# Feed-forward block of an encoder layer: TensorE's and SyncE's orders fixed in the second product, last sends behind its first loads, the block's pool split in three

## The chip, the cores and the metric

The kernel runs on one core of a Trainium2 chip. The core has five engines, each with its own in-order stream of instructions: PE (TensorE, matrix products), DVE (VectorE), ACT (ScalarE), POOL (GpSimd) and SP (SyncE, which here issues most DMA transfers). They meet only at semaphores. The metric is the device time of one launch in microseconds (us); lower is better. Before the change it is 2614.06 us, the median of 3 runs (2613.95 to 2615.7).

## What is computed

One layer of a bidirectional encoder trunk on 1024 rows of width 1024: a two-branch mixer, cross-attention into memory tokens, and a dense SwiGLU feed-forward block, each followed by a normalised residual. Only the end of the second part and the third part are touched:

```python
    x = x + _rms_norm(_memory_attention(h, mem_n, w_mq, w_mkv, w_mo), mem_post_norm)
    h = _rms_norm(x, ffn_pre_norm)
    gate, up = jnp.split(h @ w_ffn_in, 2, axis=-1)          # 1024 -> 2 * 2816
    x = x + _rms_norm((jax.nn.silu(gate) * up) @ w_ffn_out, ffn_post_norm)   # 2816 -> 1024
```

All of it is float32. A float32 product is made of three matmuls of a rounded type: each operand is split into a high part (a cast on ACT, tiles `act_hi`, `w_hi`) and the rest (a subtraction on DVE, `act_lo`, `w_lo`), and hi*hi + hi*lo + lo*hi is summed in PSUM.

## The kernel before

**End of the attention.** `phase_rest` calls `phase_mem`, whose last step is the projection by `w_mo` (`out_proj`, pool "op2"): eight row tiles, a normalisation, the residual, then the next normalisation, and transposes (L1068) that write the block's input as `hraw` (L1070). Weights `w_mo` are loaded on SP (L114), cast on POOL (L115) and subtracted on DVE (L116).

**First product (`ffn_in`).** 22 groups of 256 columns (`InGroup`): 11 of the gate, 11 of the up half. Each group is a seven-product (Strassen-like) form of a 2x2 block product, methods `p1` to `p7` (matmuls L1378, L1380, L1381). `load` (L1402) fetches a group's weights as two halves of 512 KB into a ring of three (`w_raw`, tag "wr"), `form` makes hi (L1409, ACT) and lo (L1410, DVE). `p4` adds into the PSUM tile of `p7`, so it must come after DVE has read that tile (`u2`, L1465). `send` (sums L1514 to L1521, DMAs L1519 and L1522) writes a finished group's activations and their Strassen sums to DRAM (`afA`, `afS`).

**Second product (`OutProduct`).** Seven products, n = 0 to 6, each of 11 steps g, each step with 4 output row tiles j and 3 matmuls a tile (L1636): 132 matmuls a product, 924 in all. `operands(n, g)` loads an activation tile (L1619, 256 KB from `af`) and one to three weight tiles (L1590), and makes hi and lo (L1623 to L1626, pinned). Product 6 is written last, tile by tile (33 matmuls each); its operands are made beside those of product 4. `use` adds a finished product to what is kept (L1678), squares the result on ACT with a row sum (`square`, L1649) and multiplies it by the norm's gain (`gain`, L1653). `roots` (L1661 to L1667) makes the reciprocal roots of the row sums, `write` (L1673) adds the residual row tile `xf` and stores it (L1674). `square` writes its squares into the tile `xf` and then loads the rows of `x2` over them (L1650).

**What sets the order.** A scheduler places the instructions of each engine by its own estimate of times. Instructions given to `keep_in_program_order` (`pin`) keep the order in which the program wrote them on their engine. Before, those are the casts, subtractions, adds, squares, gains, roots and writes of the second product; its matmuls and its DMAs are free. `ahead(4)` writes the first four operand sets before the last group's `p7`, and `ffn_in` ends with `prev.p4()` and `prev.p3()` of the last group. All tiles of the block lie in one pool ("ffn"): tag "t" with 36 slots, tag "tl" with 12, tag "wr" with 3.

Of the kernel before, what the change touches and what calls it, by code (L numbers as in the profile page):

```python
# [10 lines left out]
F32 = mybir.dt.float32  # L11
# [8 lines left out]
P = 128  # L20
# [1338 lines left out]


def ffn_tile(K, name, dt=F32, tag="t", bufs=36):
    return K.fp.tile([P, 512], dt, tag=tag, name=name, bufs=bufs)


def ffn_part(K):
# [15 lines left out]
        nc.tensor.matmul(out, a[k][1], b[k][0], start=False, stop=(k == n - 1), skip_group_check=True)  # L1381


class InGroup:


# [8 lines left out]

    def load(self):
        K = self.K
        self.raw = []
        for kh in range(2):
            raw = K.fp.tile([P, 4, 256], F32, tag="wr", name="w_raw", bufs=3)  # L1400
            src = K.i["w_ffn_in"][0][kh * 512:(kh + 1) * 512, self.c0:self.c0 + 256]
            K.nc.sync.dma_start(raw, src.rearrange("(k p) n -> p k n", p=P))  # L1402
            self.raw.append(raw)

    def form(self, name, src):
        K, nc = self.K, self.K.nc
# [72 lines left out]
def ffn_in(K, hf, finish, ahead):  # L1479
# [88 lines left out]
    prev.p4()  # L1568
    prev.p3()


class OutProduct:

# [11 lines left out]
    def pin(self, ins):  # L1585
        return self.K.tc.keep_in_program_order(ins)

    def weight(self, g, r, c):
        t = ffn_tile(self.K, "w_raw")
        self.K.nc.sync.dma_start(t, self.wo[g * 256 + r * P:g * 256 + (r + 1) * P, c * 512:(c + 1) * 512])  # L1590
        return t

    def second(self, name, g):
# [39 lines left out]
    def step(self, ps, n, j, g):  # L1633
        a, b = self.ops[n, g]
        js = slice(j * P, (j + 1) * P)
        mm = lambda x, y, s, e: self.K.nc.tensor.matmul(ps, x[:, js], y, start=s, stop=e, skip_group_check=True)  # L1636
        mm(a[0], b[0], g == 0 and n in (0, 2, 4), False)
        mm(a[0], b[1], False, False)
        mm(a[1], b[0], False, g == self.NG - 1)

    def square(self, src, t, ch):

        K = self.K
        g = t if t < 4 else 4
        if g not in self.ssq:
            self.ssq[g] = K.small.tile([P, 8], F32, tag="ssqo", name="ssqo", bufs=5)
        x = self.xt[t, ch] = half_tile(K, "xf")
        at = ch if t < 4 else ch * 4 + t - 4
        self.pin(K.nc.scalar.activation(x, src, AF.Square, accum_out=self.ssq[g][:, at:at + 1]))  # L1649
        K.nc.sync.dma_start(x, K.x2[t * P:(t + 1) * P, ch * 512:(ch + 1) * 512])  # L1650

    def gain(self, dst, src, ch):
        self.pin(self.K.nc.vector.tensor_mul(dst, src, self.post[ch]))  # L1653
# [16 lines left out]
    def write(self, t, r):  # L1670
        for ch in range(2):
            o = self.xt[t, ch]
            self.pin(self.K.nc.vector.scalar_tensor_tensor(o, self.acc[t // 4, ch, t % 4], r, o, op0=ALU.mult, op1=ALU.add))  # L1673
            self.K.nc.sync.dma_start(self.out[t * P:(t + 1) * P, ch * 512:(ch + 1) * 512], o)  # L1674

    def add(self, name, ps, other):
        t = half_tile(self.K, name)
# [3 lines left out]
    def use(self, n, j, ps):  # L1681
        K = self.K
        if n == 0:
            self.p1[j] = half_tile(K, "p1")
            self.pin(K.nc.scalar.copy(self.p1[j], ps))
        elif n == 1:
            self.square(ps, j, 0)
            self.acc[0, 0, j] = half_tile(K, "c11")
            self.gain(self.acc[0, 0, j], ps, 0)
        elif n == 2:  # L1690
            self.u1[j] = self.add("u1", ps, self.p1[j])
        elif n == 3:
            self.u2[j] = self.add("u2", ps, self.p1[j])
        elif n == 4:
            c = self.acc[1, 1, j] = self.add("c22", ps, self.u2.pop(j))
            self.square(c, 4 + j, 1)
            self.gain(c, c, 1)
        elif n == 5:
            c = self.acc[1, 0, j] = self.add("c21", ps, self.p1.pop(j))
            self.square(c, 4 + j, 0)  # L1700
            self.gain(c, c, 0)
        else:
            c = self.acc[0, 1, j] = self.add("c12", ps, self.u1.pop(j))
            self.square(c, j, 1)
            self.gain(c, c, 1)

    def run(self):
        K, nc = self.K, self.K.nc
        self.post = [half_tile(K, "post") for _ in range(2)]
        for ch in range(2):  # L1710
            nc.sync.dma_start(self.post[ch], K.i["ffn_post_norm"][:, ch * 512:(ch + 1) * 512].to_broadcast([P, 512]))
        sets = [[b(K) for b in (pmm, pmm, pg, ptr)], [b(K) for b in (pmm, pg, pg, ptr)]]
        of = (0, 0, 1, 1, 0, 1, 0)
        for n in range(6):
# [2 lines left out]
                ps = sets[0] = [b(K) for b in (pmm, pmm, pg, ptr)]  # L1717
            for g in range(self.NG):
                self.operands(n, g)
                if n == 4:  # L1720
                    self.operands(6, g)
                for j in range(4):
                    self.step(ps[j], n, j, g)

                if n and g == 5 and of[n - 1] != of[n]:
                    for j in range(4):
                        self.use(n - 1, j, sets[of[n - 1]][j])
            if n < 5 and of[n + 1] == of[n]:
                for j in range(4):
                    self.use(n, j, ps[j])  # L1730
# [4 lines left out]
        for j in range(4):  # L1735
# [7 lines left out]
        self.use(6, 1, ps[1])  # L1743
        self.write(1, self.roots(1, 1))
        self.write(7, r[:, 3:4])
        for j in range(2, 4):
            self.use(6, j, ps[j])
            self.write(j, self.roots(j, 1))


def phase_rest(K, out, attn, started):
    with pool(K, "sm2") as K.small, pool(K, "act") as K.ap:
# [12 lines left out]
        with pool(K, "wring", "right") as K.wp:  # L1765
# [14 lines left out]
        with pool(K, "ffn", "right") as K.fp:  # L1780
            second = OutProduct(K, out)
            ffn_in(K, sink, finish, lambda: second.ahead(4))
            second.run()


@with_exitstack
# [71 lines left out]
```

## Time and profile before

| | |
|---|---|
| median of 3 runs | 2614.06 us |
| the profiled execution | 2617.22 us |
| its span (first to last instruction) | 2615.5 us |
| granted clock, mean over the span | 0.978 of full |
| PE busy | 2468.3 us (94%) |
| DVE / ACT / POOL busy | 1789.3 / 1067.0 / 455.6 us |
| moved by DMA | 267.34 MB, 102 GB/s over the span |

The profile is one execution taken by the hardware profiler, so its spans are compared with 2617.22 us, not with the median. A busy PE is the time in which a matmul was under way; matmuls are pipelined, and back to back one of 128x512 starts every 0.23 us while its record is 0.39 us long. The granted clock has two levels in a short stretch, 1 (2.4 GHz) and 0.5 (1.2 GHz); a mean between says how much of the stretch had which. "[3.59 <-POOL w_hi L115]" behind a row means that the engine stood idle for 3.59 us before it, and what ended the wait.

### The profile page before, as it was taken

To read this page: it belongs to the slowest core of one execution; us is meant where nothing else is said; L and a number is where in the kernel's file an instruction comes from. 1 tells how busy PE (TensorE), PEld (TensorE's weight loads), DVE (VectorE), ACT (ScalarE), POOL (GpSimd) and SP (SyncE) were. 2 spreads that over 40 slices of the span, in tenths; PEclk is the share of its full clock that TensorE was granted. 3 is DMA by queue.
4 is the path that set the end of the run, shared out by engine and by line. 5 is a ranking of instruction groups with operands and counts; after the bars stand their busy time and mean duration, and the time that the engine had idled before them with its cause. 6 is when DMAs were issued, how large, how long until landed. Compare 5 with 4: busy or idle time off the path is not lost.

```text
span 2615.5 us, 38677 instructions
## 1 busy us (share of the span) xinstructions
PE 2468.3 (94%) x13445; PEld 2014.8 (77%) x13445; DVE 1789.3 (68%) x4223; ACT 1067.0 (41%) x2817; POOL 455.6 (17%) x730
## 2 busy tenths in 40 slices
PE   7999999999999999999999999999869999998993
PEld 5687778788788877788877878887658888886782
DVE  7778787887788754856576566436567666645756
ACT  5336244554554534744461233233443233324431
POOL 3351111111112111422233123213100000000000
PEclk9999999999999999999999999999989999998997
DMA  6213322322331322412124233214223323327843
GB/s 198 89 53 110 84 55 67 97 66 60 101 79 43 88 73 89 129 59 83 41 65 143 83 113 100 94 46 148 97 85 119 120 91 107 105 89 255 294 160 113
DMA packets 291757, 267.34 MB, mean 102 GB/s; under 512 B 92992, under 2 KB 213609, under 8 KB 291561
## 3 DMA queue, kind: packets, MB, share of 16 engines
q1 hardware_dynamic: 289257, 256.48, 31.4%
q10 hardware_dynamic: 2304, 8.39, 0.8%
q8 instruction: 106, 1.74, 0.3%
q14 instruction: 90, 0.74, 0.1%
HBM read 201.04 MB, written 63.77 MB: 101 GB/s over the span
## 4 chain that ended last, share of the span: by engine, by line
PE 50%; DVE 5%; DMA 2%; ACT 2%; issue 1%; POOL 1%; SPq 0%; POOLq 0%; ACTq 0%; DVEq 0%
PE mm L133 6%; PE mm L134 6%; PE mm L131 6%; PE mm L1636 3%; PE g L1378 2%; PE g L1380 2%; PE g L1381 2%; PE g L1636 2%; PE tr L904 2%; PE tr L1636 2%; PE tr L1380 1%; PE tr L1381 1%; PE tr L1378 1%; PE mm L1381 1%; PE mm L1378 1%; PE mm L1380 1%
## 5 line engine op out<-in xcount | busy, mean ns | idle before, releaser
L134 PE MATMUL mm<-act_hi,w_lo 128*128 128x512 f32 (+1 forms) x1216 | 481.5, 398 | 0.0
L133 PE MATMUL mm<-act_lo,w_hi 128*128 128x512 f32 (+1 forms) x1216 | 478.7, 396 | 0.0
L131 PE MATMUL mm<-act_hi,w_hi 128*128 128x512 f32 (+1 forms) x1216 | 333.6, 400 | 1.9 <-POOL w_hi L115 1.2
L134 PEld LDWEIGHTS mm<-act_hi,w_lo 128*128 128x128 f32 x1216 | 230.0, 189 | 37.3
L133 PEld LDWEIGHTS mm<-act_lo,w_hi 128*128 128x128 f32 x1216 | 229.9, 189 | 37.3
L131 PEld LDWEIGHTS mm<-act_hi,w_hi 128*128 128x128 f32 x1216 | 221.6, 191 | 42.8 <-POOL w_hi L115 2.0
L115 POOL TENSOR_SCALAR w_hi<-w_raw 128x512 fp32r<-128x512 f32 x232 | 161.6, 713 | 416.5 <-PE mm L133 221.6
L116 DVE TENSOR_TENSOR w_lo<-w_raw,w_hi 128x512 fp32r<-128x512 f32 x232 | 182.0, 804 | 63.5 <-POOL w_hi L115 56.7
L133 PE MATMUL mm<-w_lo,act_hi 128*128 128x512 f32 (+1 forms) x480 | 180.7, 382 | 0.0
L134 PE MATMUL mm<-w_hi,act_lo 128*128 128x512 f32 (+1 forms) x480 | 180.2, 381 | 0.0
L861 POOL TENSOR_SCALAR Pm<-Pm,sm 128x1024 f32<-128x1024 f32 (+1 forms) x96 | 89.4, 933 | 250.4 <-DVE sm L860 86.5
L459 DVE SCALAR_TENSOR_TENSOR acc<-xp,ccol,acc 128x1024 f32<-128x1024 f32 x96 | 124.0, 1292 | 4.7 <-ACT acc L456 3.8
L131 PE MATMUL mm<-w_hi,act_hi 128*128 128x512 f32 (+1 forms) x480 | 120.4, 386 | 5.1 <-POOL w_hi L115 4.0
L1409 ACT CAST w_hi<-s 128x512 fp32r<-128x512 f32 x88 | 54.1, 622 | 158.2 <-PE g L1380 101.5
L159 ACT CAST th<-tr 128x512 fp32r<-128x512 f32 x128 | 74.9, 589 | 105.2 <-PE tr L904 103.2
L133 PEld LDWEIGHTS mm<-w_lo,act_hi 128*128 128x128 f32 x480 | 91.4, 191 | 17.2
L134 PEld LDWEIGHTS mm<-w_hi,act_lo 128*128 128x128 f32 x480 | 91.4, 190 | 17.1
L131 PEld LDWEIGHTS mm<-w_hi,act_hi 128*128 128x128 f32 x480 | 86.1, 191 | 23.6 <-POOL w_hi L115 4.9
L160 DVE TENSOR_TENSOR tl<-tr,th 128x512 fp32r<-128x512 f32 x128 | 87.2, 684 | 17.5 <-ACT th L159 15.6
L857 ACT ACTIVATE Pm<-sc,nm 128x512 f32<-128x512 f32 x128 | 87.2, 690 | 16.7 <-DVE nm L852 16.3
L850 DVE TENSOR_REDUCE mx<-sc 128x1 f32<-128x512 f32 x128 | 85.0, 681 | 4.3 <-PE sc L134 4.2
L1625 DVE TENSOR_TENSOR act_lo<-a_raw,act_hi 128x512 fp32r<-128x512 f32 x77 | 52.8, 686 | 50.6 <-ACT act_hi L1623 47.1
(447 smaller groups left out, 5857.6 us busy)
## 6 DMA issues: line engine op xcount, KB each, us to landing
w_raw<-in_w_in SPq DMA_DIRECT2D x120, 256.0 KB, 3.3
w_raw<-in_w_ffn_in SPq DMA_DIRECT2D x50, 512.0 KB, 3.5
w_raw<-in_w_ffn_out SPq DMA_DIRECT2D x99, 256.0 KB, 5.3
Gr<-grow SPq DMA_DIRECT2D x48, 256.0 KB, 3.4
afS<-as SPq DMA_DIRECT2D x44, 256.0 KB, 2.1
a_raw<-afS SPq DMA_DIRECT2D x44, 256.0 KB, 4.7
afA<-sg SPq DMA_DIRECT2D x33, 256.0 KB, 2.0
a_raw<-afA SPq DMA_DIRECT2D x33, 256.0 KB, 5.1
```

Of the source, the lines that this page charges most:

```text
L115: nc.gpsimd.tensor_scalar(hi[part], raw, 1.0, 1.0, op0=ALU.mult, op1=ALU.mult)
L116: nc.vector.tensor_sub(lo[part], raw, hi[part].bitcast(F32))
L131: nc.tensor.matmul(out, a[0], b[0], start=(i == 0), stop=False)
L133: nc.tensor.matmul(out, a[0], b[1], start=False, stop=False)
L134: nc.tensor.matmul(out, a[1], b[0], start=False, stop=(i == n - 1))
L160: nc.vector.tensor_sub(lo, ps, hi.bitcast(F32))
L459: nc.vector.scalar_tensor_tensor(acc, xp[:, j:j + T], tap(j), acc, op0=ALU.mult, op1=ALU.add)
L861: nc.gpsimd.tensor_scalar(Pm, Pm, sm[:, 0:1], 1.0, op0=ALU.mult, op1=ALU.mult)
L1378: nc.tensor.matmul(out, a[k][0], b[k][0], start=(start and k == 0), stop=False, skip_group_check=True)
L1380: nc.tensor.matmul(out, a[k][0], b[k][1], start=False, stop=False, skip_group_check=True)
L1381: nc.tensor.matmul(out, a[k][1], b[k][0], start=False, stop=(k == n - 1), skip_group_check=True)
L1636: mm = lambda x, y, s, e: self.K.nc.tensor.matmul(ps, x[:, js], y, start=s, stop=e, skip_group_check=True)
```

## The change

It does seven things. (1) The second product's matmuls and all its loads and stores on SP are pinned. (2) The pool is split: "ffe" holds the ring "wr" and is opened before the `w_mo` projection, "ffl" holds tag "tl", "ffn" the rest. (3) The first three weight halves of `ffn_in` are loaded ahead, before `out_proj` is written. (4) `a_raw` of the second product moves from the 36 slots of "t" to the 3 slots of "wr". (5) The last group's `send` and the gain loads `post` are written at n = 0, g = 6. (6) The residual rows `xf` are loaded by `rows` at the end of the program, no longer by `square`; the squares go to a junk tile. (7) The gains of products 4 and 5 come after all four adds, product 6's gain writes a tile of its own, and product 6's operands are spread over n = 4 and n = 5.

```diff
 def ffn_tile(K, name, dt=F32, tag="t", bufs=36):
-    return K.fp.tile([P, 512], dt, tag=tag, name=name, bufs=bufs)
+    return (K.fp if tag == "t" else K.fl).tile([P, 512], dt, tag=tag, name=name, bufs=bufs)
...
+def weight_half(K, c0, kh):
+    raw = K.fe.tile([P, 4, 256], F32, tag="wr", name="w_raw", bufs=3)
...
+        self.raw = [K.pre.pop((self.c0, kh), None) or weight_half(K, self.c0, kh) for kh in range(2)]
...
-            if (r, c) == (0, 1):
+            if (r, c) == (0, 1) and g < NG - 1:
                 send(g)
...
+    return lambda: send(NG - 1)
...
+    def load(self, to, src):
+        self.pin(self.K.nc.sync.dma_start(to, src))
...
-        ar = ffn_tile(K, "a_raw")
-        nc.sync.dma_start(ar, K.af[first][g])
+        ar = K.fe.tile([P, 4, 256], F32, tag="wr", name="a_raw", bufs=3).rearrange("p a b -> p (a b)")[:, 0:512]
+        self.load(ar, K.af[first][g])
...
-        mm = lambda x, y, s, e: self.K.nc.tensor.matmul(ps, x[:, js], y, start=s, stop=e, skip_group_check=True)
+        mm = lambda x, y, s, e: self.pin(self.K.nc.tensor.matmul(ps, x[:, js], y, start=s, stop=e, skip_group_check=True))
...
+    def rows(self, t):
+        for ch in range(2):
+            x = self.xt[t, ch] = ffn_tile(self.K, "xf", F32, "tl", 12)
+            self.load(x, self.K.x2[t * P:(t + 1) * P, ch * 512:(ch + 1) * 512])
...
-            self.gain(c, c, 1)
-    def run(self):
+            self.acc[0, 1, j] = half_tile(K, "g12")
+            self.gain(self.acc[0, 1, j], c, 1)
+    def use_all(self, n, ps):
+        for j in range(4):
+            self.use(n, j, ps[j])
+        if n > 3:
+            for j in range(4):
+                self.gain(self.acc[1, 5 - n, j], self.acc[1, 5 - n, j], 5 - n)
+    def run(self, send):
...
                 self.operands(n, g)
-                if n == 4:
-                    self.operands(6, g)
+                if n == 0 and g == 6:
+                    send()
+                    self.post = [half_tile(K, "post") for _ in range(2)]
+                    for ch in range(2):
+                        self.load(self.post[ch], K.i["ffn_post_norm"][:, ch * 512:(ch + 1) * 512].to_broadcast([P, 512]))
+                if n == 4 and g > 3:
+                    self.operands(6, g - 4)
+                if n == 5 and g in (4, 6, 8, 10):
+                    self.operands(6, 5 + g // 2)
...
-        for j in range(4):
-            self.use(5, j, sets[1][j])
+        self.use_all(5, sets[1])
+        for t in (4, 5, 0, 6, 1, 7):
+            self.rows(t)
...
+            fe = ExitStack()
+            K.fe = fe.enter_context(pool(K, "ffe"))
+            K.pre = {(c0, kh): weight_half(K, c0, kh) for c0, kh in ((0, 0), (0, 1), (DFF, 0))}
             with pool(K, "op2") as op:
```

On SP, around the loads of `w_mo`, the program before has (columns: line, operation, written tile and source, shape, count):

```order
L1001 DMA a_raw<-oM_84 128x512 x2
L114 DMA w_raw<-in_w_mo 128x512 x5
L1137 DMA post<-in_mem_post_norm 128x1024
L114 DMA w_raw<-in_w_mo 128x512 x4
L1145 DMA xr<-x_88 128x1024
L114 DMA w_raw<-in_w_mo 128x512 x4
L1145 DMA xr<-x_88 128x1024
```

and now:

```order
L1001 DMA a_raw<-oM_84 128x512 x2
L114 DMA w_raw<-in_w_mo 128x512 x5
L1388 DMA w_raw<-in_w_ffn_in 128x4x256 x3
L114 DMA w_raw<-in_w_mo 128x512 x4
L1137 DMA post<-in_mem_post_norm 128x1024
L114 DMA w_raw<-in_w_mo 128x512 x4
L1145 DMA xr<-x_88 128x1024
```

The three loads of the feed-forward block stand between the fifth and the sixth load of `w_mo`, and `post` stands behind the ninth.

On PE, where the first product ends, the program before has (tile `g` written by `p7`, last four rows of it, then the second product's first step):

```order
L1380 MATMUL g<-part,w_hi 128x512
L1381 MATMUL g<-part,w_lo 128x512
L1380 MATMUL g<-part,w_hi 128x512
L1381 MATMUL g<-part,w_lo 128x512
L1636 MATMUL mm<-w_hi,act_hi 128x512
L1636 MATMUL mm<-w_lo,act_hi 128x512
L1636 MATMUL mm<-w_hi,act_lo 128x512
L1636 MATMUL mm<-w_hi,act_hi 128x512
```

and now, after the same end of `p7`, with numbers (`w_hi_23202` is `p7`'s weight, `w_hi_23206` is `p4`'s):

```order
L1380 MATMUL g_23230<-part_19993,w_hi_23202 128x512
L1381 MATMUL g_23230<-part_19992,w_lo_23203 128x512
L1378 MATMUL g_23230<-part_19994,w_hi_23206 128x512
L1378 MATMUL g_23230<-part_19996,w_hi_23206 128x512
L1378 MATMUL g_23230<-part_19899,w_hi_23206 128x512
L1378 MATMUL g_23230<-part_19901,w_hi_23206 128x512
L1380 MATMUL g_23230<-part_19995,w_hi_23206 128x512
```

`p4` and `p3` (24 matmuls) now stand straight behind `p7`, ahead of the whole second product; before, 40 rows of the second product's steps 0 to 3 stood between `p7` and `p4`.

At the end of PE's stream the program before has (`tr_24597` is the last tile of product 6, `mm_23410`, `g_23411`, `g_23412` and `tr_23413` the four of product 5):

```order
L1636 MATMUL tr_24597<-w_hi_24962,act_hi_24960 128x512
L1636 MATMUL tr_24597<-w_lo_24963,act_hi_24960 128x512
L1636 MATMUL tr_24597<-w_hi_24962,act_lo_24961 128x512
L1636 MATMUL mm_23410<-w_hi_25247,act_hi_25245 128x512
L1636 MATMUL g_23411<-w_hi_25247,act_hi_25245 128x512
L1636 MATMUL g_23412<-w_hi_25247,act_hi_25245 128x512
L1636 MATMUL tr_23413<-w_hi_25247,act_hi_25245 128x512
```

and now, where product 5 ends (`tr_23400` is its last tile, `mm_24596` product 6's first):

```order
L1644 MATMUL tr_23400<-w_hi_25259,act_hi_25257 128x512
L1644 MATMUL tr_23400<-w_lo_25260,act_hi_25257 128x512
L1644 MATMUL tr_23400<-w_hi_25259,act_lo_25258 128x512
L1644 MATMUL mm_24596<-w_hi_24704,act_hi_24702 128x512
L1644 MATMUL mm_24596<-w_lo_24705,act_hi_24702 128x512
L1644 MATMUL mm_24596<-w_hi_24704,act_lo_24703 128x512
```

Before, product 6 was drawn forward among product 5's steps, and both ended together; now all 132 matmuls of product 6 stand behind product 5's last, one row tile after another.

## Rows read from the trace of the kernel before

**Rows 1.** Windows: start and end, us, busy by engine (count), PEclk, DMA share, GB/s

```profile
1950.00:2338.00 388.00, 386.00 (x1701) 318.46 (x1700) 259.54 (x409) 120.59 (x203) 0.00 (x0) 1.00 0.30 102
...
2385.00:2391.00 6.00, 4.39 (x13) 3.50 (x14) 4.93 (x9) 6.00 (x13) 0.00 (x0) 0.75 0.50 161
...
2448.00:2455.00 7.00, 4.46 (x15) 3.26 (x14) 6.67 (x12) 2.42 (x5) 0.00 (x0) 0.84 1.04 382
...
2574.30:2615.50 41.20, 0.18 (x1) 0.00 (x0) 29.88 (x91) 5.36 (x16) 0.00 (x0) 0.56 0.42 153
```

**Rows 2.** Timeline, the end: start, us, engine, line, operation, tiles [idle before <-releaser]

```profile
2574.09 0.39 PE L1636 MATMUL tr<-w_hi,act_lo 128*128 128x512 f32 x1
...
2573.16 0.69 DVE L1678 TENSOR_TENSOR c<-mm,p 128x512 f32<-128x512 f32 x1 [9.59 <-PE mm L1636]
...
2583.91 2.74 DVE L1673 SCALAR_TENSOR_TENSOR xf<-c,ro,xf 128x512 f32<-128x512 f32 x4
...
2606.56 0.68 DVE L1678 TENSOR_TENSOR c<-tr,u 128x512 f32<-128x512 f32 x1
2608.09 0.69 DVE L1653 TENSOR_TENSOR c<-c,post 128x512 f32<-128x512 f32 x1 [0.85 <-ACT xf L1649]
2608.70 0.15 DVE L1661 TENSOR_TENSOR ro<-ssqo 128x1 f32<-128x1 f32 x1
...
2611.78 0.99 SPq L1674 DMA_DIRECT2D out<-xf  x2
```

**Rows 3.** Timeline of SP, PE and DVE where the second product starts

```profile
2336.41 0.32 SPq L1519 DMA_DIRECT2D afA<-sg  x1
2336.82 0.38 SPq L1619 DMA_DIRECT2D a_raw<-afA  x1
...
2339.22 0.39 SPq L1590 DMA_DIRECT2D w_raw<-in_w_ffn_out  x1
...
2359.25 0.39 SPq L1619 DMA_DIRECT2D a_raw<-afA  x1
...
2338.22 0.39 PE L1636 MATMUL mm<-w_hi,act_hi 128*128 128x512 f32 x1
...
2359.06 0.79 PE L1636 MATMUL mm<-w_lo,act_hi 128*128 128x512 f32 x1 [4.01 <-DVE w_lo L1626]
...
2384.41 0.39 PE L1636 MATMUL tr<-w_hi,act_lo 128*128 128x512 f32 x1
...
2345.65 0.68 DVE L1465 TENSOR_TENSOR u<-g,p 128x512 f32<-128x512 f32 x1
```

**Rows 4.** Timeline of POOL and PE at the sixth load of w_mo

```profile
1784.63 3.29 POOL L115 TENSOR_SCALAR w_hi<-w_raw 128x512 fp32r<-128x512 f32 x4 [3.93 <-DMA w_raw<-in_w_mo]
...
1785.30 0.79 PE L131 MATMUL mm<-w_hi,act_hi 128*128 128x512 f32 x1 [3.59 <-POOL w_hi L115]
```

**Rows 5.** Timeline of PE and ACT where the first product starts

```profile
1889.20 1.54 PE L1068 MATMUL tr<-ident,y 128*128 128x128 f32 x6 [8.36 <-POOL y L1030]
...
1893.77 1.65 ACT L1409 CAST w_hi<-w_raw 128x512 fp32r<-128x512 f32 x3
...
1901.63 0.62 ACT L1409 CAST w_hi<-w_raw 128x512 fp32r<-128x512 f32 x1 [0.93 <-DMA w_raw<-in_w_ffn_in]
...
1905.83 0.60 ACT L1492 ACTIVATE sg<-mm 128x512 f32<-128x512 f32 x1 [1.79 <-PE mm L1381]
```

**Rows 6.** Timeline of PE where product 1 and product 3 start

```profile
2386.61 0.73 PE L1636 MATMUL mm<-w_hi,act_hi 128*128 128x512 f32 x2 [1.81 <-ACT w_hi L1624]
...
2451.41 0.50 PE L1636 MATMUL mm<-w_hi,act_hi 128*128 128x512 f32 x1 [2.54 <-ACT w_hi L1624]
```

**Rows 7.** Page, DMA issues: tiles, queue, operation, count, KB each, us to landing

```profile
w_raw<-in_w_ffn_out SPq DMA_DIRECT2D x99, 256.0 KB, 5.3
...
a_raw<-afS SPq DMA_DIRECT2D x44, 256.0 KB, 4.7
...
a_raw<-afA SPq DMA_DIRECT2D x33, 256.0 KB, 5.1
```

More of the change, by code (lines that the diff above doesn't have):

```diff
@@ L1381, in mmk @@
         nc.tensor.matmul(out, a[k][1], b[k][0], start=False, stop=(k == n - 1), skip_group_check=True)
+def weight_half(K, c0, kh):
+    raw = K.fe.tile([P, 4, 256], F32, tag="wr", name="w_raw", bufs=3)
+    src = K.i["w_ffn_in"][0][kh * 512:(kh + 1) * 512, c0:c0 + 256]
+    K.nc.sync.dma_start(raw, src.rearrange("(k p) n -> p k n", p=P))
+    return raw
 class InGroup:
@@ L1397, in load @@
         K = self.K
[L1398 to L1403, printed above, removed]
+        self.raw = [K.pre.pop((self.c0, kh), None) or weight_half(K, self.c0, kh) for kh in range(2)]
     def form(self, name, src):
@@ L1586, in pin @@
         return self.K.tc.keep_in_program_order(ins)
+    def load(self, to, src):
+        self.pin(self.K.nc.sync.dma_start(to, src))
     def weight(self, g, r, c):
         t = ffn_tile(self.K, "w_raw")
-        self.K.nc.sync.dma_start(t, self.wo[g * 256 + r * P:g * 256 + (r + 1) * P, c * 512:(c + 1) * 512])
+        self.load(t, self.wo[g * 256 + r * P:g * 256 + (r + 1) * P, c * 512:(c + 1) * 512])
         return t
@@ L1673, in write @@
             self.pin(self.K.nc.vector.scalar_tensor_tensor(o, self.acc[t // 4, ch, t % 4], r, o, op0=ALU.mult, op1=ALU.add))
-            self.K.nc.sync.dma_start(self.out[t * P:(t + 1) * P, ch * 512:(ch + 1) * 512], o)
+            self.load(self.out[t * P:(t + 1) * P, ch * 512:(ch + 1) * 512], o)
     def add(self, name, ps, other):
@@ L1700, in use @@
             self.square(c, 4 + j, 0)
-            self.gain(c, c, 0)
         else:
-            c = self.acc[0, 1, j] = self.add("c12", ps, self.u1.pop(j))
+            c = self.add("c12", ps, self.u1.pop(j))
             self.square(c, j, 1)
-            self.gain(c, c, 1)
-    def run(self):
+            self.acc[0, 1, j] = half_tile(K, "g12")
[7 more added lines that the diff above has]
+    def run(self, send):
         K, nc = self.K, self.K.nc
-        self.post = [half_tile(K, "post") for _ in range(2)]
-        for ch in range(2):
-            nc.sync.dma_start(self.post[ch], K.i["ffn_post_norm"][:, ch * 512:(ch + 1) * 512].to_broadcast([P, 512]))
         sets = [[b(K) for b in (pmm, pmm, pg, ptr)], [b(K) for b in (pmm, pg, pg, ptr)]]
@@ L1725, in run @@
                 if n and g == 5 and of[n - 1] != of[n]:
-                    for j in range(4):
-                        self.use(n - 1, j, sets[of[n - 1]][j])
+                    self.use_all(n - 1, sets[of[n - 1]])
             if n < 5 and of[n + 1] == of[n]:
-                for j in range(4):
-                    self.use(n, j, ps[j])
+                self.use_all(n, ps)
         ps = sets[0]
@@ L1734, in run @@
                 self.step(ps[j], 6, j, g)
-        for j in range(4):
-            self.use(5, j, sets[1][j])
+        self.use_all(5, sets[1])
+        for t in (4, 5, 0, 6, 1, 7):
+            self.rows(t)
         r = self.roots(4, 4)
@@ L1745, in run @@
         self.write(7, r[:, 3:4])
+        self.rows(2)
+        self.rows(3)
         for j in range(2, 4):
@@ L1779, in phase_rest @@
                 finish = out_proj(K, op, wb, om, "mem_post_norm", K.x1, K.x2, sink)
-        with pool(K, "ffn", "right") as K.fp:
+        with pool(K, "ffn", "right") as K.fp, pool(K, "ffl") as K.fl:
             second = OutProduct(K, out)
-            ffn_in(K, sink, finish, lambda: second.ahead(4))
-            second.run()
+            second.run(ffn_in(K, sink, finish, lambda: second.ahead(4)))
+        fe.close()
 @with_exitstack
```

4 lines of the change are left out of this document (1 added, 3 removed).

## Prediction, written before the changed kernel was run

> **What bounds the kernel now.** I read the windows first, then the timelines of PE, DVE and SP at the places where a window shows PE idle, then the landing times of the loads. PE is the bound: through most of the first product it is busy 386 of 388 us at full clock, and 388 us hold 1701 matmuls, 0.228 us each [rows 1]. So a microsecond is won only where PE has nothing to run, and the reader is to see four such places. The largest is the end: the last matmul starts at 2574.09 and is over by 2574.48 [rows 2], the span ends at 2615.5, and in between DVE works 29.88 of 41.20 us [rows 1]. It waited 9.59 us for product 5 and then had everything left to do [rows 2]. The second is the start of the second product: 132 matmuls of product 0 and 24 of `p4` and `p3` lie between 2338.22 and 2384.64 [rows 3]; 156 x 0.228 = 35.6, so 10.8 of 46.4 us are lost, because step 5's load went out only at 2359.25 [rows 3], behind the last sends. The third is the start of the first product, where PE waits 8.36 us for POOL and no weight of the block is cast before 1893.77 [rows 5]. The fourth is the sixth load of `w_mo`, 3.59 us [rows 4].
>
> **The end.** In the new order product 5 ends, then PE runs product 6 for 132 x 0.228 = 30.1 us, tile by tile in 7.5 us, and product 5's adds, roots and writes lie beside it. What follows PE's end is one row tile. Before, such a tile took from its add at 2606.56 to the span's end at 2615.5, 8.9 us; its gain stood between square and roots (2608.09 to 2608.70, 0.6 us) and now stands beside the square [rows 2]. So 8.3 us, and 0.1 for the wait on PE, against 2615.5 - 2574.48 = 41.0: **-32.6**. This holds if DVE keeps up. From product 5's end I count, with 0.61 from one add or gain to the next, four adds and four gains (5.0, with the last square's way), roots 2.4 (as from 2608.70 to the write), two row tiles written 2.7, so +10.1 us; then the blocks of rows 0, 1 and 2, which before took from 2583.91 + 2.74 = 2586.65 to 2606.56, 19.9 us, and now 0.6 less each, 18.1: +28.2 [rows 2]. Product 6's last tile is ready at +30.1, so 1.9 us are to spare. If each block took 1 us more, the end would come 1.1 us later. The twelve residual loads, 3.1 MB, are 8 us at the 382 GB/s of [rows 1] and lie behind the last operand loads, in front of product 6's 30 us, which need none.
>
> **The start of the second product.** The late loads go: steps 4 to 6 are fetched ahead of most of the sends. But a new wait comes. `p4` is now PE's next instruction after `p7`, and it overwrites the tile that DVE's `u2` reads; on DVE `u2` still stands behind the pinned subtractions of steps 0 to 3. Before, it ran at 2345.65 while PE had steps 0 to 3 to do [rows 3]. Those subtractions wait for the loads issued from 2336.82 to 2339.22 [rows 3]; one of them now goes out before the send, so the rest come 0.48 us earlier. I expect `u2` over at 2345.65 - 0.48 + 0.68 = 2345.85 and PE idle from 2338.22, 7.6 us. Queued behind the waiting `p4` is all of the second product, and nothing else can run on PE. After an idle 1.81 us the 13 matmuls from 2386.61 to 2391 took 4.4 us instead of 3.0, at clock 0.75 [rows 1, 6], so I add 1.4. Then 7.6 + 1.4 - 10.8 = **-1.8**. Bounds: nothing waits (-10.8) to loads that land 3 us later (+1.2); I take the value nearest the rows.
>
> **Products 1 and 3.** These starts wait for ACT's first cast, 1.81 and 2.54 us [rows 6], since DVE and ACT first evacuate the product before; that stays. Before, four matmuls with `w_hi` and `act_hi` ran first; in program order the second matmul needs `w_lo` too, one subtraction later (0.69). The four that ran beside it are delayed by part of that: **+0.8** for both (0 to +1.4).
>
> **The loads ahead of `w_mo`.** Three loads of 512 KB now stand before the sixth load of `w_mo`, whose cast already ended PE's wait [rows 4]; `post` (512 KB) moves from before it to behind the ninth. Net 1.05 MB at 382 GB/s [rows 1] is **+2.7**. Bounds: 0.5, if the queue has slack, and 4.5, if all three loads go in front and `post` had been free.
>
> **The start of the first product.** With weights present, ACT casts and DVE subtracts them before the last normalisation, and PE has 24 matmuls of groups 0 and 1 for its idle 8.36 us. On DVE three subtractions of 0.68 [rows 3] stand in the normalisation's chain, 2.0 us. The transposes' copies were over when the casts began at 1893.77 [rows 5]; now near 1895.8, where `p2` of group 0 starts; its 12 matmuls take 2.7. Its `sg` came at 1905.83, after weights cast at 1901.63 that had waited for DMA [rows 5]; now near 1898.8, 7.0 us earlier. The sums that follow on DVE and ACT move with it: **-7.0**. Bounds: -3, if these sums are ordered behind something that does not move, and -9.5, if the chain is not lengthened.
>
> **Three slots for `a_raw`.** A load can go out when the subtraction of the load three before is done. Landing 4.7 to 5.3 [rows 7], cast 0.62 [rows 5], subtraction 0.68: 6.6 us for three steps of 12 x 0.228 = 2.74, that is 8.2. Hidden, nothing added; in product 4 from g = 4 on there are two such loads a step, three slots are 1.5 steps = 4.1 us, and 7 steps could each lose (6.6 - 4.1) / 1.5 = 1.7 us, 12 in all, less the lead gained before. I take 0, and keep up to 8 for the range.
>
> The Trainium skill has a rule against this change ("DMA: Bandwidth & Descriptors", section "Where 436 GB/s comes from"): loads from HBM into a core are held by about 358 GB/s. Product 2 needs four loads of 256 KB a step, and by that rule 1.05 MB would take 2.93 us, so pinned steps would add 11 x 0.19 = 2.1 us. The trace moved 382 GB/s from 2448 to 2455 [rows 1]; at that rate a step needs 2.74 us, PE's own pace, so I add nothing.
>
> **Sum.** -32.6 - 1.8 + 0.8 + 2.7 - 7.0 = -37.9. The profiled execution took 2617.22, so 2579.3; the median is 3.16 below it: **2576 us**.
>
> **Rivals.**
> A, no new wait: `u2` comes by itself early, because DVE's four pairs are not as late as before. For it: the first step's subtractions were done before PE got there at 2338.22. Against it: the fourth step's weight cannot go out before 2338 and needs some 5 us to land [rows 7]. Then the start gives -10.8: 2567 us.
> B, the idle place before the first product is not filled: what bounds it is the chain of sums on ACT and DVE, and the new loads cost their full 4.5. For it: that chain alone ended in waits of PE far behind 1905. Against it: its first member is `sg`, which waited for PE. 2576 + 7.0 + 1.8 = 2585 us; with the three slots' loss 2593.
> C, slower than before: pinned PE waits at every step for an operand, since loads run only three ahead. It loses the whole gain if each of 66 steps costs 37.9 / 66 = 0.57 us, that is when landing, cast and subtraction pass 3 x (2.74 + 0.57) = 9.9 us. Measured 6.6 with many transfers in flight. From there on over 2614; at 11 us of landing and work, 0.93 a step, 2638 us.
> D, the new order does not shorten the end, since DVE falls behind. With its blocks as long as before, 10.1 + 19.9 = 30.0 is still within the 30.1 us of product 6; so I fold D into the forecast.
>
> **Chances.** Forecast 0.57 (its own range 2570 to 2583), A 0.16, B 0.22, C 0.05. The range takes A and B in, the ends of the unknown costs with them: 2562 to 2592. A difference under 0.2%, about 5 us, is one that a measurement of this kernel can't tell from none. Faster 0.95, within 0.2% 0.01, slower 0.04.
>
> **What would show it.** PE's records end with product 6's last tile, and the span ends 8 to 9 us behind; if DVE's last add starts later than 0.5 us after PE's end, the count of blocks was wrong. PE idle some 7 us where the second product starts (near 2334, 4 us ahead of before), ended by DVE `u2`: the new wait; without it A. `w_mo`'s sixth cast waits 6 to 7 us on DMA instead of 3.93. The first matmul of the first product lies before the last transposes, and `sg` comes 7 us nearer to them. In product 4, casts that wait for `a_raw` while PE waits for the cast would show the three slots. The prediction is wrong if the time is above 2592, which would mean that pinned PE waits at many steps, or below 2562.

## The result, and the profile after

The changed kernel takes 2572.47 us (median of 3 runs, 2571.03 to 2572.9) against 2614.06: ratio 0.984, 95% interval 0.982 to 0.986. Forecast was 2576 with a range of 2562 to 2592. The profiled execution has a span of 2570.7 us; PE is busy 2462.7 us of it (96%).

The change was worth most at the end. The timelines of PE, DVE and SP there answer to [rows 2] (start, us, engine, line, operation, tiles, idle before and its releaser):

```profile
2547.43 0.69 DVE L1690 TENSOR_TENSOR c<-mm,u 128x512 f32<-128x512 f32 x1 [0.32 <-PE mm L1644]
...
2554.91 0.69 DVE L1690 TENSOR_TENSOR c<-g,u 128x512 f32<-128x512 f32 x1 [0.93 <-PE g L1644]
...
2560.43 0.75 DVE L1685 SCALAR_TENSOR_TENSOR xf<-c,ro,xf 128x512 f32<-128x512 f32 x1 [1.69 <-DMA xf<-x]
...
2561.96 0.39 PE L1644 MATMUL tr<-w_hi,act_lo 128*128 128x512 f32 x1
...
2562.39 0.69 DVE L1690 TENSOR_TENSOR c<-tr,u 128x512 f32<-128x512 f32 x1 [0.54 <-PE tr L1644]
...
2566.86 0.75 DVE L1685 SCALAR_TENSOR_TENSOR xf<-g,ro,xf 128x512 f32<-128x512 f32 x1
...
2555.56 1.86 SPq L1594 DMA_DIRECT2D xf<-x  x4
2561.21 6.75 SPq L1594 DMA_DIRECT2D out<-xf  x4
```

PE ends at 2562.35 and the span 8.35 us later; before it was 41.0. The last three of DVE's four adds for product 6 wait for PE (0.32, 0.93, 0.54 us), so DVE keeps up, one tile behind. The wait at 2560.43 is for a residual row whose load went out only at 2555.56, behind twelve stores; it left 0.54 us to spare.

The second product's start, which answers to [rows 3]: PE, DVE and SP.

```profile
2330.55 0.39 PE L1381 MATMUL g<-part,w_lo 128*128 128x512 f32 x1
2337.54 2.07 PE L1378 MATMUL g<-part,w_hi 128*128 128x512 f32 x4 [6.60 <-DVE u L1468]
...
2345.69 0.39 PE L1644 MATMUL mm<-w_hi,act_hi 128*128 128x512 f32 x1
...
2336.19 0.69 DVE L1634 TENSOR_TENSOR w_lo<-w_raw,w_hi 128x512 fp32r<-128x512 f32 x1 [0.42 <-ACT w_hi L1632]
2336.80 0.68 DVE L1468 TENSOR_TENSOR u<-g,p 128x512 f32<-128x512 f32 x1
...
2353.49 0.32 SPq L1525 DMA_DIRECT2D afS<-as  x1
```

The new wait of `p4` is there: 6.60 us. It lasts until `u2` (2336.80), which stands behind the fourth pair of subtractions on DVE. Behind it four matmuls take 2.07 us, where four such took 1.07 at full clock 9 us earlier; the granted clock of these 5.28 us is 0.50 (window, columns as in the table of windows below):

```profile
2337.54:2342.82 5.28, 5.28 (x12) 4.13 (x13) 1.36 (x2) 0.54 (x1) 0.00 (x0) 0.50 0.14 53
```

After that PE waits for nothing until product 1.

The first product's start, which answers to [rows 4, 5]: POOL, PE and ACT (the row of 1784.65 is the sixth load of `w_mo`, that of 1878.69 the last matmul with `w_mo`).

```profile
1783.98 3.42 POOL L115 TENSOR_SCALAR w_hi<-w_raw 128x512 fp32r<-128x512 f32 x4 [6.05 <-DMA w_raw<-in_w_mo]
...
1784.65 0.80 PE L131 MATMUL mm<-w_hi,act_hi 128*128 128x512 f32 x1 [5.71 <-POOL w_hi L115]
...
1878.69 0.39 PE L134 MATMUL mm<-w_hi,act_lo 128*128 128x512 f32 x1
...
1892.36 1.42 PE L1068 MATMUL tr<-ident,y 128*128 128x128 f32 x6 [2.07 <-POOL y L1030]
...
1881.63 1.65 ACT L1412 CAST w_hi<-w_raw 128x512 fp32r<-128x512 f32 x3
...
1898.79 0.60 ACT L1495 ACTIVATE sg<-mm 128x512 f32<-128x512 f32 x1 [2.25 <-PE mm L1381]
```

The casts stand 12 us earlier than before, PE's long wait before the last transposes is 2.07 us and not 8.36, and the cast of the sixth load of `w_mo` waits longer for its DMA, 6.05 us where it was 3.93.

Windows (start and end, us, busy by engine PE, PEld, DVE, ACT, POOL with count, PEclk, DMA share, GB/s): the starts of products 1 and 3, the first two in the kernel before, the last two in the kernel after.

```profile
2386.61:2392.61 6.00, 6.00 (x19) 4.80 (x20) 6.00 (x11) 6.00 (x12) 0.00 (x0) 0.72 0.68 223
2451.41:2457.41 6.00, 6.00 (x19) 4.79 (x20) 5.67 (x9) 3.25 (x6) 0.00 (x0) 0.72 1.04 384
...
2377.49:2383.49 6.00, 5.69 (x24) 4.49 (x25) 4.50 (x8) 3.86 (x7) 0.00 (x0) 1.00 0.63 198
2440.24:2446.24 6.00, 5.77 (x17) 4.38 (x18) 5.69 (x10) 3.38 (x7) 0.00 (x0) 0.72 0.79 248
```

In the kernel after the first rows wait 1.71 and 2.03 us, before 1.81 and 2.54. The clock stayed full behind the first (1.00) and fell behind the second (0.72); before, it fell behind both.

### The profile page after: what moved, and what is told of

The parts are those of the page before. It is cut to its first block, busy times and chain, and to the rows that moved or that the text cites. A ratio compares the mean times of both kernels' runs of the same rounds, so it can differ in the third digit from the quotient of the medians.

```text
span 2570.7 us, 38670 instructions
## 1 busy us (share of the span) xinstructions
PE 2462.7 (96%) x13445; PEld 2010.6 (78%) x13445; DVE 1791.1 (70%) x4223; ACT 1068.5 (42%) x2817; POOL 458.2 (18%) x730
## 5 line engine op out<-in xcount | busy, mean ns | idle before, releaser
L643 DVE TENSOR_TENSOR Ly<-Ly,tmp 128x240 f32<-128x240 f32 (+27 forms) x248 | 82.4, 332 | 3.2
```

## The experiments

**How the terms are compared.** Two executions don't reach the `w_mo` stage at the same time, though the code ahead of it is the same: the same transposes of the attention start at 1750.24 us in the profile of the kernel after and at 1759.79 in that of a_raw_in_36 below, whose profiled execution, 2585.36 us, is the longest of its four. So each term is taken inside a profile. The columns: the wait at the sixth load of `w_mo`; from the end of the last `w_mo` matmul to the start of the first `sg`; from there to PE's end; from PE's end to the span's end, the tail (us). The label stands for the kernel of that experiment.

| kernel | 6th load | to `sg` | `sg` to PE's end | tail | median | ratio to before, interval |
|---|---|---|---|---|---|---|
| before | 3.59 | 27.64 | 668.65 | 41.02 | 2614.06 | |
| after | 5.71 | 19.71 | 663.56 | 8.35 | 2572.47 | 0.984 (0.982 to 0.986) |
| pe_free | 5.57 | 19.71 | 661.51 | 19.97 | 2583.86 | 0.988 (0.987 to 0.990) |
| u2_first | 4.34 | 19.69 | 658.39 | 8.30 | 2567.71 | 0.983 (0.981 to 0.984) |
| late_prefetch | 2.87 | 20.56 | 664.42 | 8.28 | 2572.55 | 0.984 (0.982 to 0.985) |
| no_prefetch | 3.38 | 20.37 | 664.30 | 8.26 | 2570.75 | 0.983 (0.982 to 0.985) |
| ring_in_pool | 1.92 | 21.40 | 663.43 | 8.28 | 2573.6 | 0.984 (0.983 to 0.985) |
| one_pool | 1.47 | 28.79 | 663.23 | 8.34 | 2577.42 | 0.986 (0.984 to 0.987) |
| before_split | 1.91 | 21.92 | 667.43 | 40.99 | 2606.74 | 0.997 (0.996 to 0.998) |
| send_first | 5.32 | 19.71 | 663.78 | 8.30 | 2574.9 | 0.985 (0.983 to 0.986) |
| a_raw_in_36 | 5.74 | 19.59 | 666.33 | 8.31 | 2576.91 | 0.986 (0.984 to 0.987) |
| n4_pinned | 4.90 | 19.67 | 665.26 | 8.35 | 2573.82 | 0.984 (0.983 to 0.986) |
| no_prefetch_u2_first | 2.89 | 20.88 | 659.08 | 8.29 | 2566.56 | 0.981 (0.980 to 0.983) |

The kernel before, beside them, had medians of 2613.37 (pe_free to no_prefetch), 2615.35 (ring_in_pool, send_first, a_raw_in_36, no_prefetch_u2_first) and 2614.27 (one_pool, before_split, n4_pinned); so differences of 2 us between medians of different groups say nothing, and of the changed kernel's relatives only pe_free has an interval apart from its. The columns of the profiles decide, each of one execution. How far they move by themselves shows where an edit doesn't reach: from `sg` to PE's end the five kernels whose edits lie ahead of it (after, late_prefetch, no_prefetch, ring_in_pool, one_pool) take 663.22 to 664.42.

**The end: PE's order.** In pe_free the matmuls of the second product are not pinned, the loads are.

```diff
-        mm = lambda x, y, s, e: self.pin(self.K.nc.tensor.matmul(...))
+        mm = lambda x, y, s, e: self.K.nc.tensor.matmul(...)
```

> The changed kernel with the pin taken off the second product's matmuls alone; loads, prefetch, sends and operands as changed. The scheduler then writes p4 behind 43 step rows again, and draws the first two row tiles of product 6 in among product 5's steps, so that product 5's last matmul stands 72 rows (16.4 us) ahead of PE's last instead of 132 (30 us). Theory (the end is as long as what DVE still has to do when PE ends: some 37 us from product 5's end, or one row tile, 8.35, whichever is later): 37.3 - 16.4 = 20.9 us behind PE's end instead of 8.35, +12.5; the wait of p4 (6.60 and its half-speed restart, some 8.5 in all) goes; together +4, about 2576 us. Rival (the order of products 5 and 6 is not what shortened the end, the later residual loads are): the end stays 8 to 9 us, -8.5, about 2564. Second rival (the pin itself gives everything): back to some 2605.

Measured 2583.86. DVE, PE and SP at the end of it:

```profile
2547.56 0.69 DVE L1690 TENSOR_TENSOR c<-mm,p 128x512 f32<-128x512 f32 x1 [11.68 <-PE mm L1644]
...
2575.86 0.75 DVE L1685 SCALAR_TENSOR_TENSOR xf<-c,ro,xf 128x512 f32<-128x512 f32 x1 [1.71 <-DMA xf<-x]
...
2565.04 0.39 PE L1644 MATMUL tr<-w_hi,act_lo 128*128 128x512 f32 x1
...
2576.63 6.11 SPq L1594 DMA_DIRECT2D out<-xf  x4
```

DVE gets product 5 at 2547.56, 17.9 us before PE's end and not 31.9 (2530.43 after), since parts of product 6 were drawn forward again. The tail grows from 8.35 to 19.97 us, 11.6 where the first theory had 12.5; the 1.71 us for a residual row, which PE's pace hides in the changed kernel, lie in it. From `sg` to PE's end only 2.0 us are won and not 8.5: the wait of `p4` is gone, but a stall on a late load takes its place, and so the time is 2583.86 and not 2576:

```profile
2367.39 0.80 PE L1644 MATMUL mm<-w_hi,act_hi 128*128 128x512 f32 x1 [5.28 <-ACT w_hi L1632]
```

The later residual loads and the moved gains were not run apart from PE's order. From product 5's first add to the span's end DVE's chain takes 42.3 us in the kernel before (2573.16 to 2615.5) and 37.9 in pe_free, so by my estimate PE's order alone would leave a tail of 42.3 - 31.9 = 10.4 us, and these edits have up to 2 us of the 32.7.

**The new wait: u2 on DVE.** In u2_first the four operand sets are written behind the last `p7`, so that `u2` stands ahead of their subtractions.

```diff
-        if G is groups[-1]:
-            ahead()
-            G.last = True
+        G.last = G is groups[-1]
         G.p7()
+        if G.last:
+            ahead()
```

> The changed kernel with the first four operand sets written behind the last p7 and its use, so that u2 stands ahead of their subtractions on DVE; PE's order is the same row by row. Theory (p4 waits only because u2 stands behind these subtractions): PE's wait of 6.60 us and the half-speed restart (some 1.9) go, -8.5, about 2564 us; up to 2 us less if the sends that now stand between the loads make a step late. Rival (the real limit is the landing of the loads of steps 1 to 3): the wait moves from p4 to steps 1 to 3, and the time stays at 2572.

PE in it:

```profile
2332.40 1.20 PE L1378 MATMUL g<-part,w_hi 128*128 128x512 f32 x4 [0.78 <-DVE u L1468]
...
2359.10 0.49 PE L1643 MATMUL mm<-w_hi,act_hi 128*128 128x512 f32 x1 [1.91 <-ACT w_hi L1631]
```

The wait falls from 6.60 to 0.78 us and the four matmuls from 2.07 to 1.20; then a step waits 1.91 us for a later load. Net -5.2 us from `sg` to PE's end, -4.8 of the median, where theory had 8.5. So the wait was what bounded this place, with a little of the old stall behind it.

**The loads ahead of `w_mo`.** In late_prefetch they are written at the fourth row tile of the projection, behind all loads of `w_mo`; in no_prefetch not at all, so that the groups ask for them (its edit is shown).

```diff
 # no_prefetch
-            K.pre = {(c0, kh): weight_half(K, c0, kh) for c0, kh in ((0, 0), (0, 1), (DFF, 0))}
+            K.pre = {}
```

> The changed kernel with the three prefetched weight loads written into the projection's loop at its fourth row tile; on SP they stand behind all 16 loads of w_mo instead of behind the fifth. Theory (the prefetch delays the sixth load of w_mo and so costs some 3.8 us in that stage, measured from the first load of w_mo to its last matmul): PE's wait there returns from 5.71 to about 3.6, the start of the first product stays as changed, -3.8, about 2569 us. Rival (the 3.8 are a drift between two executions and the queue had slack): 2572, within 1.

> The changed kernel without the three prefetched loads; they are issued when the groups ask for them, the ring still in a pool of its own that is open during the projection. Theory: the gain at the start of the first product (8.2 us) goes and the cost at w_mo (3.8 us) too, +4.4, about 2577 us. Rival A (a pool of its own lets the scheduler issue the loads early all the same, once the ring is free): the gain stays and the cost goes, about 2569. Rival B (the prefetch bought nothing): 2568 to 2570 with the first matmul of the first product behind the last transposes.

The sixth load's wait falls to 2.87 and 3.38 us. Over all profiles, the six with loads ahead of it wait 5.26 us in the mean (4.34 to 5.74), the seven without 2.58 (1.47 to 3.59): 2.7 us. The whole stage, from the transposes named above to the end of the last `w_mo` matmul, shows more: 127.8 to 129.5 us in the six, 123.8 to 126.1 in the seven, 4.0 between the means; the rest is smaller waits and clock (granted 0.96 to 0.97 in the six, 1.00 in three of the seven). The start of the first product hardly moves, 0.9 and 0.7 us later, where my theory had some 7 for no_prefetch. But this does not show that early loads are worth nothing, for in no_prefetch, as its rival A had it, they still go out 85 us before their first cast (1878.43):

```profile
1792.92 1.53 SPq L1388 DMA_DIRECT2D w_raw<-in_w_ffn_in  x3
```

The two runs show that a place ahead of the sixth `w_mo` load costs three to six times what it brings over one behind them all. The medians are those of the changed kernel within the noise, so what is saved at `w_mo` shows in the profiles alone. What brought the 7.9 us between 27.64 and 19.71 the next runs ask.

**The ring's place, then all tiles in one pool, then the split alone.** In ring_in_pool the ring lies in the block's pool again; in one_pool tag "tl" does too; in before_split the kernel before gets only the pool "ffl" for tag "tl". Nothing is loaded ahead in the three.

```diff
 # ring_in_pool
-            K.fe = fe.enter_context(pool(K, "ffe"))
+            K.fe = K.fp
 # one_pool
-        with pool(K, "ffn", "right") as K.fp, pool(K, "ffl") as K.fl:
+        with pool(K, "ffn", "right") as K.fp:
+            K.fe = K.fl = K.fp
 # before_split, on the kernel before
-        with pool(K, "ffn", "right") as K.fp:
+        with pool(K, "ffn", "right") as K.fp, pool(K, "ffl") as K.fl:
-    return K.fp.tile([P, 512], dt, tag=tag, name=name, bufs=bufs)
+    return (K.fp if tag == "t" else K.fl).tile([P, 512], dt, tag=tag, name=name, bufs=bufs)
```

> The ring of the first product's weights is put back into the block's pool, as before, and nothing is loaded ahead; all else as in the changed kernel. Theory (where the ring lies is what brought the start of the first product forward): the first load of the block again waits for the last w_mo matmul, it goes out near 1878 and not near 1793, PE idles some 8 us before the last transposes, and the time is that of the kernel without loads ahead plus the 8.2 us that the start had won: 2570.8 + 8.2 = 2579. The sixth w_mo load loses nothing any more (3.6 us of wait, as before). Rival (the 8.2 us come from elsewhere, from the pinned loads or the split pools as such): the start stays where it is and the time stays at 2571.

> The changed kernel with all of the block's tiles in one pool again, as before, and nothing loaded ahead; the pinned orders, the late sends, the late rows stay. Theory (the split alone brought the first product forward): 27.6 us from the last w_mo matmul to the first sg, the casts again behind the last copies of hraw, and 6 us above the kernel with the ring alone put back (2573.6 beside 2615.35 of before, ratio 0.984): ratio about 0.9865, 2578 to 2580. Rival (the split doesn't matter): ratio 0.984, 2573.

> The kernel before with one thing of the change alone: tag tl (12 slots) lies in a pool of its own, the rest of the block's pool stays as it was, ring and all. Theory (where the block's tiles lie decides when the first product may start: with 12 slots fewer in the large pool the first casts needn't stand behind the last normalisation on ACT): from the last w_mo matmul to the first sg 21 to 22 us and no longer 27.6, PE has matmuls of the first groups between the last transposes, and the time is about 6 us below the kernel before, 2608. Rival (the pinned orders of the second product shift the scheduler's estimates, and the split only stands beside it): 27.6 us from matmul to sg, and the time of the kernel before, 2614.

ring_in_pool refuted its theory, that the ring's place brought the start forward: 21.40 us to `sg`, 1.0 more than no_prefetch, and not 8. Its SP and ACT:

```profile
1871.01 26.65 SPq L1388 DMA_DIRECT2D w_raw<-in_w_ffn_in  x9
...
1881.65 0.60 ACT L1412 CAST w_hi<-w_raw 128x512 fp32r<-128x512 f32 x1
```

The first loads go out at 1871, as in the kernel before, where SP's row (of all nine loads to 1903) and the last copies on ACT are

```profile
1870.12 33.26 SPq L1402 DMA_DIRECT2D w_raw<-in_w_ffn_in  x9
...
1892.19 1.69 ACT L1070 ACTIVATE hraw<-tr,cols 128x256 f32<-128x256 f32 x4 [0.48 <-PE tr L1068]
```

and the cast at 1881.65 waits for nothing. So the weights were there in time before the change as well (the page of the kernel before gives these loads a median of 3.5 us from issue to landing, and the cast comes some 24 us behind the first issue); the first casts merely stood behind the last copies of `hraw` in ACT's order. one_pool and before_split say what decides that order. one_pool, PE and ACT:

```profile
1884.96 1.54 PE L1068 MATMUL tr<-ident,y 128*128 128x128 f32 x6 [8.37 <-POOL y L1030]
...
1889.53 1.65 ACT L1412 CAST w_hi<-w_raw 128x512 fp32r<-128x512 f32 x3
...
1902.73 0.60 ACT L1495 ACTIVATE sg<-mm 128x512 f32<-128x512 f32 x1 [2.83 <-PE mm L1381]
```

before_split, PE and ACT:

```profile
1876.17 1.20 PE L1378 MATMUL mm<-act_hi,w_hi 128*128 128x512 f32 x4 [0.56 <-ACT w_hi L1409]
...
1884.79 1.54 PE L1068 MATMUL tr<-ident,y 128*128 128x128 f32 x6 [1.31 <-POOL y L1030]
...
1875.51 0.60 ACT L1409 CAST w_hi<-w_raw 128x512 fp32r<-128x512 f32 x1
...
1894.88 0.60 ACT L1492 ACTIVATE sg<-mm 128x512 f32<-128x512 f32 x1 [1.84 <-PE mm L1381]
```

With one pool the wait (8.37 us, 8.36 before) and the late casts are back, with all the pinned orders of the change in place. With the split alone, on the kernel before, the first cast starts 2.6 us behind the end of the last `w_mo` matmul and not 15.6, and 5.7 us are won to `sg` (7.5 of the median). Moving 12 slots out of the large pool does it, shown in both directions. That the first casts' tiles then no longer lie over tiles that the projection still uses is my reading of why the scheduler may place them earlier; it was not measured apart. Loads that go out at 1871 and not at 1775 cost 1.7 us of the start (21.40 and 19.71), so most of the 7.9 is the split's.

**Sends ahead of the loads.** In send_first the last group's sends are written where they were before.

```diff
-            if (r, c) == (0, 1) and g < NG - 1:
+            if (r, c) == (0, 1):
                 send(g)
...
-    return lambda: send(NG - 1)
+    return lambda: None
```

> The last group's sends are written where they were before, ahead of the second product's loads; all else as in the changed kernel. Theory (the late loads were cured by PE's order, since p4 and p3 now finish before step 0, so the sums that the sends wait for are there early): steps 4 to 6 lose at most 1 us, 2572.5 to 2573.5. Rival (writing the sends behind the loads is what won the 10.8 us): SP stands in a send while the loads of step 4 and later wait behind it, PE waits again some 9 us in product 0, 2581.

SP and PE in it:

```profile
2350.56 1.65 SPq L1522 DMA_DIRECT2D afS<-as  x3
2352.49 0.32 SPq L1525 DMA_DIRECT2D afS<-as  x1
2352.90 0.41 SPq L1594 DMA_DIRECT2D a_raw<-afA  x1
...
2340.36 2.07 PE L1378 MATMUL g<-part,w_hi 128*128 128x512 f32 x4 [7.27 <-DVE u L1468]
...
2379.98 0.50 PE L1644 MATMUL mm<-w_hi,act_hi 128*128 128x512 f32 x1 [1.71 <-ACT w_hi L1632]
```

The loads of the later steps go out only at 2352.90 and PE still waits for none of them: `p4`'s wait, `p4` and `p3` stand between the last `p7` and step 0, where before step 0 followed at once. It takes 0.2 us more from `sg` to PE's end, which is within what that column moves by itself. So the old stall was cured by `p4` and `p3` in front, not by the sends' place.

**Three slots, and product 6's operands.** a_raw_in_36 puts `a_raw` back into tag "t"; n4_pinned makes product 6's operands beside product 4 alone.

```diff
 # a_raw_in_36
-        ar = K.fe.tile([P, 4, 256], F32, tag="wr", name="a_raw", bufs=3).rearrange(...)[:, 0:512]
+        ar = ffn_tile(K, "a_raw")
 # n4_pinned
-                if n == 4 and g > 3:
-                    self.operands(6, g - 4)
-                if n == 5 and g in (4, 6, 8, 10):
-                    self.operands(6, 5 + g // 2)
+                if n == 4:
+                    self.operands(6, g)
```

> The second product's activation loads go back into the 36 slots, from the ring of three; all else as in the changed kernel. Theory (three slots are hidden): 2572.5, no difference above 1.5 us. Rival (three slots hold up loads somewhere): faster by 2 to 8 us, with the waits of PE at the starts of products 1 and 3 shorter. A second rival (the move made room in the 36 slots): slower by 2 us or more, with loads of w_raw that wait for a slot.

> Product 6's operands are all made beside product 4, one set a step, as before; PE's order and all else as in the changed kernel. Theory (the spread costs and brings nothing, since PE nowhere waits in products 4 and 5): 2572.5, within 1.5 us. Rival (a step of product 4 then needs five loads and two casts and subtractions more, and pinned PE can't go on to other work): PE waits at steps of product 4, 0.5 us each, and up to 5 us are lost, 2577.

With `a_raw` among the 36, 2.8 us are lost from `sg` to PE's end: `p4` waits 8.16 (6.60 to 7.27 in the other kernels with `p4` in front and `u2` behind) and a row of product 5 waits for its cast, which none does in the changed kernel.

```profile
2349.20 2.08 PE L1378 MATMUL g<-part,w_hi 128*128 128x512 f32 x4 [8.16 <-DVE u L1468]
...
2530.31 0.50 PE L1644 MATMUL mm<-w_hi,act_hi 128*128 128x512 f32 x1 [0.61 <-ACT w_hi L1632]
```

From product 3's first row to PE's end it takes 124.05 us, where seven of the other kernels take 122.1. SP's waits (line, releaser, us in total, times, longest), first the changed kernel from 2345.7 to 2532.2, then a_raw_in_36 from 2356.5 to 2545:

```profile
SPq L1594 <- PE tr L1644: 11.3, 13, 4.6
...
SPq L1594 <- PE tr L1644: 70.9, 29, 8.7
```

The loads wait for tiles that PE still reads. That bears out the second rival: the move made room. n4_pinned lost 1.7 us in its profile, 0.8 beyond what the column moves by itself, and its median can't be told from the changed kernel's; PE waits at no step of product 4 in it, so its rival did not come.

**The version with the lowest time.** no_prefetch_u2_first joins two edits shown above.

> Nothing loaded ahead, the ring in its own pool, and u2 ahead of the first four operand sets. Theory (the two act at different places and add up): 2570.8 - 4.8 = 2566, with PE's wait at the second product's start under 1 us and 3.4 us at the sixth w_mo load; best of all so far, and more than 45 us below the kernel before. Rival (u2's gain is eaten by the later loads, as half of it was): 2570.

2566.56 us, ratio 0.981, the lowest of all: 4.5 us less from `sg` to PE's end and 2.8 less at the sixth load than the changed kernel, 1.2 more to `sg`. Beside it, on the same chip, three relatives of the changed kernel took 2573.6 to 2576.91. u2_first alone comes within its interval, and its interval and the changed kernel's still touch (0.982 to 0.983); that it is the faster of the two rests on the profiles (2565.1 and 2570.7 us).

## Why the prediction was right, and where it was not

In the profiles 44.8 us are gone (2615.5 to 2570.7), 41.6 of the medians; forecast was 37.9. Of the 44.8, 3.2 lie ahead of the `w_mo` stage, where the code is the same (its transposes start at 1753.42 and 1750.24), and say nothing of the change. The rest, in the order of the program: +4.1 in the `w_mo` stage, -7.9 to the first `sg`, -0.4 in the first product, -1.6 at the second product's start, -3.1 from product 1 to PE's end, -32.7 in the tail, -41.6 together. The forecast is 3.7 us short: 3.9 and 0.9 us too little gain in two terms, and against them 1.4 too little cost in one.

*The end*: -32.7 measured, -32.6 forecast. Its reasons hold too: pe_free brings the tail back by nearly the amount worked out (11.6 of 12.5 us), and DVE waits for PE and not the other way. What I overlooked is that only twelve of the sixteen residual loads find a slot ahead of product 6. The last four go out at 2555.56, behind stores, and DVE's spare time at the last add fell from some 2.2 us (as in send_first, where that add waits 2.20 us for PE) to 0.54; I had 1.9.

*The start of the second product*: -1.6, forecast -1.8. The wait of 7.6 us was 6.6 by its row and 7.0 from the last matmul's start; twelve matmuls at half clock, from 2337.54 to 2342.82, took 5.3 us and not 2.7, so that cost 2.5 where I had 1.4. The 10.8 us of before had two causes, and I gave one. The first wait, 4.01 us for a `w_lo` [rows 3], was no late load: its cast ran 13 us earlier, and its subtraction, without a wait of its own, stood on DVE behind the send's sums.

```profile
2345.62 0.62 ACT L1624 CAST w_hi<-w_raw 128x512 fp32r<-128x512 f32 x1
...
2357.12 0.68 DVE L1521 TENSOR_TENSOR as<-sg,as 128x512 f32<-128x512 f32 x1
...
2358.32 0.68 DVE L1626 TENSOR_TENSOR w_lo<-w_raw,w_hi 128x512 fp32r<-128x512 f32 x1
```

Only the second wait of before, 1.96 us at 2366.08, hung on the load of 2359.25. In pe_free, with the sends late and `p4` not in front, the first is 0.67 us and the second 5.28. Rival A, no wait, would have won more than u2_first did: 5.2 of the 9.0, since the late loads come back as soon as PE is early. The step "the late loads go" was half right: not by the sends' place but because PE arrives later.

*Products 1 and 3*: forecast +0.8, measured -3.1 (up to PE's end); this is the term that was mis-sized. I priced the second matmul's wait for `w_lo` (0.31 and 0.23 us, right) but took the clock as it was in [rows 1]. At product 1 it stayed full, 24 matmuls in 6 us where product 3 has 17 and the kernel before had 19; and two waits of before near 2514 (0.31 and 0.23 us) are gone. Why the clock held there stays open.

*The loads ahead of `w_mo`*: +2.7 forecast. The sixth load's wait is 2.7 us longer in the means of thirteen profiles, as forecast, but the stage 4.0 us: I had priced one wait and not what follows it, the smaller waits and the clock.

*The start of the first product*: -7.0 forecast, -7.9 measured, and the cause was wrong. The step that failed is "with weights present, ACT casts and DVE subtracts them before the last normalisation": the weights had been present before. [rows 5] said so, since the cast at 1893.77 carries no wait for a DMA while the one at 1901.63 does; I read its late start as a late load. The order on ACT held it, and the split of the pool set that order free (before_split, one_pool). So that the number fits is luck. One part held: the transposes that wait for the last normalisation start 13.3 us behind `w_mo`'s end and not 11.0, 2.3 us later, where I had 2.0 for the longer chain.

*Three slots*: 0 forecast; no PE wait in product 4. The edit brought some 2 to 3 us, by the room that it left in the 36 slots, which I had not looked for.

*Rivals*: B priced a place that is not filled; one_pool is that case, and lost 28.79 - 21.40 = 7.4 us of the start. C, waits at each step, did not come. What pinning SP's loads is worth was not run apart.

The rule of the Trainium skill on loads from HBM ("DMA: Bandwidth & Descriptors", section "Where 436 GB/s comes from", some 358 GB/s) did not bear on the time: in the changed kernel PE waits at no step of product 2. The traces go above that figure, here over six microseconds in which only loads are issued (387 in the kernel before, from 2430 to 2460 us); before_split, window at the start of product 3, last column GB/s:

```profile
2439.53:2445.53 6.00, 6.00 (x19) 4.81 (x20) 5.66 (x9) 3.25 (x6) 0.00 (x0) 0.72 1.06 388
```

## What to carry to other kernels

When a row starts late, look first at whether it carries a wait: one without a releaser was held by its engine's order, as the cast at 1893.77 and the subtraction at 2358.32 were, and no earlier load will move it. Where a scheduler sets the order, which pool a tile lies in can set that order, so undo a split alone before giving its gain to the load that came with it. And pinning an order turns an engine's freedom into one wait: find what its first instruction then waits for, and write that producer early on its own engine.

## What the runs showed of the hardware that I had not expected

The same wait doesn't always cost the clock. Ahead of product 3's start PE waited 2.03 us in the changed kernel and in no_prefetch_u2_first. In the changed kernel (the window of 2440.24 above) it then ran at 0.72 and issued 17 matmuls in 6 us. no_prefetch_u2_first, windows of its starts of products 1 and 3:

```profile
2373.59:2379.59 6.00, 5.69 (x24) 4.52 (x25) 4.60 (x9) 3.89 (x7) 0.00 (x0) 1.00 0.69 211
2436.31:2442.31 6.00, 5.78 (x24) 4.55 (x25) 5.69 (x10) 3.43 (x7) 0.00 (x0) 1.00 0.81 270
```

pe_free kept full clock there too (1.00 over 2445.45 to 2451.45, 26 matmuls), after 2.46 us. So seven matmuls, 1.6 us, hang on more than the length of the wait; on what else, these runs do not tell.
